# A hybrid decoder layer on one core: one substitution for two, weight loads and subtractions moved between products

## The chip, the cores and the metric

The kernel runs on one core of a Trainium2 chip. A core has five engines that run their own instruction streams and wait for each other through semaphores: TensorE (PE in the profile; the unit that multiplies matrices, with its weight loads shown apart as PEld), VectorE (DVE), ScalarE (ACT), GpSimd (POOL) and SyncE (SP, which here issues DMAs). The metric is the device time of one execution in microseconds, the median of several runs. The kernel before has 1929.55 us, the median of three runs (1926.06, 1929.55 and 1931.4).

## The reference

One decoder layer over 1024 tokens with 1024 features, float32 throughout. Cut to its stages:

```python
u  = rmsnorm(h, norm_mix_pre)
qa, ka, va, za, ba, aa, ..., gnsa, gmix = split(u @ w_in)
ya = gdn_mixer(qa, ka, va, za, ba, aa, ...)   # chunked gated delta rule, 4 heads of 128
yb = nsa_mixer(...)                           # compressed, selected and window attention
g_a, g_b = split(sigmoid(gmix))
mixed = (g_a * (ya @ w_a2d) + g_b * (yb @ w_b2d)) @ w_o
h = h + rmsnorm(mixed, norm_mix_post)
f = causal_dwconv(rmsnorm(h, norm_ffn_pre) @ w_up) + conv_ffn_b
f_gate, f_val = split(f)
h = h + rmsnorm((gelu(f_gate) * f_val) @ w_down, norm_ffn_post)
h = h + rmsnorm((p @ w_ple) * sigmoid(h @ w_ple_gate), norm_ple_post)
```

In `gdn_mixer`, q, k and v pass a causal convolution of width 4 and a silu; q and k are normalised over each head. For every chunk and head a strictly lower triangular matrix L is formed, whose entry (i, j) is beta_i times k_i.k_j times exp(gc_i - gc_j), where gc is the running sum of the log decay. I + L is inverted (the reference solves with it), and the state runs over the chunks with the results. The kernel uses chunks of 128 tokens, eight in all, so there are 32 matrices L (eight chunks by four heads).

## The kernel before, in words

Almost every matrix product is done in three matmuls (`mm3`): each operand is kept as a rounded part hi and a remainder lo, and hi x hi, hi x lo and lo x hi are added up in PSUM. So each weight tile that is loaded by DMA (`raw`) needs two conversions before PE can use it: ACT copies it to hi, and DVE or POOL subtracts hi from raw for lo (`lo_of`, line 362). `stream` does that for the columns of a matrix, `resident` for the rows of w_o, `hl` for a tile that is in SBUF.

**The delta-net (GDN) stage**, some 60 to 285 us of the span. Twelve convolution tiles (`conv`; four of k, four of q, four of v) follow each other. Of each, PE makes 48 matmuls of 128x512 into a PSUM tile `pj`; ACT and DVE form the convolution `y` from it (one ACT pass, three DVE passes, line 573), and ACT the silu. After the q and k tiles, `norms` squares them on ACT and adds the squares over partitions by small products into `pss`. When the fourth k tile is there, `gdn_small` computes everything per token and head: beta, gc, the norms' factors, and rows of them that are spread over partitions through DRAM.

`gdn_inverse32` is a generator that is advanced once per convolution. Per chunk it scales k, calls `decay` (E = exp of the negated, clipped difference of gc: four DVE subtractions, line 948, and one ACT exponential, line 953), forms k k^T on PE (`pkk`), and L by two DVE passes (lines 984 and 985). L goes to DRAM, and its 32x32 diagonal blocks come back one on each partition (128 blocks: 32 matrices with four blocks each). All blocks are then inverted at once by forward substitution along the free axis: 31 columns, each one multiplication (line 1003) and one subtraction (line 1005). This is done in two halves: chunks 0 to 3, then their substitution on partitions 0 to 63, then chunks 4 to 7 and theirs on partitions 64 to 127. The inverses go to DRAM (`xd`), the tile is cleared (line 1011), and `gdn_prep` loads per chunk the inverted diagonal blocks and the off-diagonal blocks of L (`blk`) and builds the full inverse by products that depend on each other (`pz`, `pt` and so on).

Four gate tiles (`gate_tile`, 48 matmuls in two halves each, copied out by ACT as `yz`) come between the last convolution and `gdn_prep(0)`; sixteen more fill the scan over the chunks.

**The merge**, some 965 to 1025 us. For pairs of feature tiles f and both halves th of the tokens, PE multiplies yb by w_b2d into `pab` (`b_product`), and DVE forms ga*a + gb*b with gates read back from DRAM (`gt`). The result `mx` is kept as hi and lo. The next but one pair of w_b2d tiles is streamed at the end of each pair (its lo on POOL). Four of w_o's eight rows of tiles (`NWO`) are loaded ahead of the merge, the rest behind it. Then `token_mm` makes the output product `pwo` per tile of 128 tokens: tokens 0 to 2 with rows 0 to 3, then again with rows 4 to 7; the others all in one.

**The up- and down-projection** (1045 to 1800 us) use a scheme with seven products of half-size blocks in place of eight, with sums and differences of blocks formed by DVE and POOL. `UpProjection.rest` begins with the pairs 0 to 2 in an order written out by hand. `turn(t2s, 4, ...)` forms the operand T4 (a difference and a sum on DVE, hi on ACT, lo on DVE); `self.copied` is the last copy of a product out of PSUM by ACT, here that of the product named r (line 106). `block_sum` is a sum on POOL that the down-projection needs. In `down`, the products 0, 1, 6, 4 and 3 follow each other, each of eleven steps j with twelve matmuls (`dq`, `dm`, `dz`). Each step converts one activation tile (`whl`, lo on DVE) and one w_down tile (`wdhl`, lo on POOL). Beside product 4, DVE forms two differences per step for later products, lines 1567 and 1568.

What sets the order: the tile framework schedules each engine's instructions from the program's order and priorities; `issue_after` (and `behind`, line 1396, which nests several) puts what is issued inside it later than a named instruction in the queue of that instruction's engine. It does not wait for its end.

## Time and profile before

| | |
|---|---|
| runs | 1926.06, 1929.55, 1931.4 us; median 1929.55 |
| profiled execution | 1925.03 us, span 1923.3 us |
| mean granted clock of TensorE | 0.986 |
| busy PE, DVE, ACT, POOL | 95%, 65%, 48%, 36% of the span |
| DMA | 93 GB/s mean |

The profile's timeline gives one row per instruction or run of like instructions, with the start, the time and, in brackets, how long the engine was idle before it and what ended that. A granted clock below 1.0 in a stretch says that TensorE ran at the lower of its two levels (1.2 of 2.4 GHz) for a part of it. A name such as `pj<-uh,whi` is output from inputs; L394 is line 394.

### The profile page before, as it was taken

The numbers are of one execution on the slowest core, as the hardware profiler recorded it, in microseconds if no ns is written. First come the engines' busy times: TensorE is split into PE (matmuls) and PEld (weight loads), VectorE is DVE, ScalarE is ACT, GpSimd is POOL, SyncE is SP. The second block draws the span as 40 slices with busy tenths as digits, with TensorE's granted clock in tenths as the row PEclk, the third lists the DMA queues.
The fourth block names the chain that finished last, engine by engine and source line by source line (L and its number), as shares of the span: only waits on it lengthen the run. The fifth ranks groups of instructions, "written<-read, shape, count | busy, mean of one in ns | idle before, by whom it ended". The sixth has DMA issues, their size and how long they took to land. (4 is left out here: it accounts for less than half of the span.)

```text
span 1923.3 us, 25903 instructions
## 1 busy us (share of the span) xinstructions
PE 1834.8 (95%) x9307; PEld 1524.8 (79%) x9307; DVE 1242.5 (65%) x2353; ACT 919.2 (48%) x1817; POOL 700.2 (36%) x527
## 2 busy tenths in 40 slices
PE   7999989999999999999889998999999999899998
PEld 7888778988888888778768886787878877677786
DVE  5437934441367667766786589888777775948643
ACT  4344223323367667766664245444444444446432
POOL 2132112224122112331153146666666664645200
PEclk9999999999999999999999999999999999999999
DMA  5124333333310100110065212223332256246201
GB/s 168 34 86 116 91 92 89 93 88 92 102 45 18 45 29 34 57 44 13 22 216 169 98 55 94 98 94 101 107 99 93 99 206 243 77 138 219 76 34 44
DMA packets 182622, 178.67 MB, mean 93 GB/s; under 512 B 27549, under 2 KB 133342, under 8 KB 182494
## 3 DMA queue, kind: packets, MB, share of 16 engines
q1 hardware_dynamic: 180272, 170.33, 28.3%
q10 hardware_dynamic: 2222, 6.69, 0.9%
q8 instruction: 73, 1.20, 0.2%
q14 instruction: 55, 0.45, 0.1%
HBM read 132.65 MB, written 44.34 MB: 92 GB/s over the span
## 5 line engine op out<-in xcount | busy, mean ns | idle before, releaser
L394 PE MATMUL pj<-uh,whi 128*128 128x512 f32 x640 | 259.1, 405 | 7.4 <-DVE y L573 4.5
L395 PE MATMUL pj<-ul,whi 128*128 128x512 f32 x640 | 255.5, 399 | 0.0
L396 PE MATMUL pj<-uh,wlo 128*128 128x512 f32 x640 | 254.9, 398 | 0.0
L362 POOL TENSOR_TENSOR wlo<-raw,whi 128x1024 fp32r<-128x1024 f32 x48 | 117.5, 2449 | 312.1 <-ACT whi L373 268.3
L394 PEld LDWEIGHTS pj<-uh,whi 128*128 128x128 f32 x640 | 121.4, 190 | 35.4 <-issue 4.5
L362 POOL TENSOR_TENSOR whl<-s,whl 128x512 fp32r<-128x512 f32 x84 | 119.5, 1425 | 70.8 <-ACT whl L1393 69.0
L396 PEld LDWEIGHTS pj<-uh,wlo 128*128 128x128 f32 x640 | 121.2, 189 | 28.5
L395 PEld LDWEIGHTS pj<-ul,whi 128*128 128x128 f32 x640 | 121.4, 190 | 25.7
L362 POOL TENSOR_TENSOR whl<-raw,whl 128x512 fp32r<-128x512 f32 x71 | 114.6, 1621 | 62.6 <-ACT whl L1393 62.0
L362 POOL TENSOR_TENSOR wdhl<-wd,wdhl 128x512 fp32r<-128x512 f32 x66 | 100.0, 1524 | 82.2 <-ACT wdhl L1393 78.9
L362 DVE TENSOR_TENSOR whl<-araw,whl 128x512 fp32r<-128x512 f32 x77 | 89.8, 1173 | 54.9 <-ACT whl L1393 54.8
L394 PE MATMUL q<-mxh,whl 128*128 128x512 f32 (+1 forms) x272 | 105.9, 394 | 7.7 <-ACT r L106 7.7
L1275 ACT ACTIVATE Pt<-Pt,nm 128x640 f32<-128x640 f32 (+7 forms) x128 | 93.0, 729 | 36.4 <-DVE nm L1273 35.9
L1305 DVE TENSOR_TENSOR Tl<-pt,Th 128x512 fp32r<-128x512 f32 (+1 forms) x152 | 92.5, 616 | 21.7 <-ACT Th L1304 17.3
L396 PE MATMUL q<-mxh,whl 128*128 128x512 f32 (+1 forms) x272 | 105.1, 387 | 0.7 <-POOL whl L362 0.7
L395 PE MATMUL q<-mxl,whl 128*128 128x512 f32 (+1 forms) x272 | 105.3, 387 | 0.0
L1304 ACT ACTIVATE Th<-pt 128x512 fp32r<-128x512 f32 (+1 forms) x152 | 78.5, 539 | 42.7 <-PE po L1308 33.4
L373 ACT ACTIVATE whi<-raw 128x1024 fp32r<-128x1024 f32 x48 | 50.5, 1053 | 85.5 <-PE pj L395 55.5
L1301 PE MATMUL pt<-ident,Pt 128*128 128x128 f32 x528 | 83.4, 277 | 5.1 <-DVE Tl L1305 3.2
L1343 POOL TENSOR_TENSOR tm<-tm 128x128 f32<-128x128 f32 x32 | 14.8, 462 | 195.1 <-DVE tm L1341 155.3
L152 DVE SCALAR_TENSOR_TENSOR yg<-c,cv,yg 128x511 f32<-128x511 f32 (+2 forms) x88 | 76.9, 875 | 2.1 <-ACT yg L149 1.8
L152 DVE SCALAR_TENSOR_TENSOR yv<-c,cv,yv 128x1023 f32<-128x1023 f32 (+1 forms) x44 | 65.7, 1492 | 15.7 <-ACT yv L149 13.4
(548 smaller groups left out, 5181.4 us busy)
## 6 DMA issues: line engine op xcount, KB each, us to landing
raw<-in_w_up SPq DMA_DIRECT2D x44, 512.0 KB
raw<-in_w_in SPq DMA_DIRECT2D x40, 512.0 KB
araw<-acts SPq DMA_DIRECT2D x35, 512.0 KB
acts<-sd SPq DMA_DIRECT2D x44, 256.0 KB
gates_d<-yz SPq DMA_DIRECT2D x40, 256.0 KB
acts<-yv SPq DMA_DIRECT2D x33, 256.0 KB
gt<-gates_d SPq DMA_DIRECT2D x32, 256.0 KB
wd<-in_w_down SPq DMA_DIRECT2D x7, 1024.0 KB
```

The lines of the kernel that those rows point to most:

```text
L152: self.body.nc.vector.scalar_tensor_tensor(y, src, w, y, ALU.mult, ALU.add)
L362: return eng.tensor_sub(lo, src, hi.bitcast(F32)).ins
L373: nc.scalar.activation(hi, raw, AF.Copy)
L394: nc.tensor.matmul(ps, lh, rh, start=start, stop=False, skip_group_check=more)
L395: nc.tensor.matmul(ps, lh, rl, start=False, stop=False, skip_group_check=more)
L396: nc.tensor.matmul(ps, ll, rh, start=False, stop=stop, skip_group_check=more)
L1275: nc.scalar.activation(Pt[:, hh, 0:nk], Pt[:, hh, 0:nk], AF.Exp, scale=2.0 ** -(h0 + hh + 1), bias=nm[:, br, hh:hh + 1], accum_out=rs[:, b ...
L1301: nc.tensor.transpose(pt[:, b, hh], Pt[:, hh, (b0 + b) * P:(b0 + b + 1) * P], self.ident)
L1304: nc.scalar.activation(Th[:, 0:m], pt[:, 0:m], AF.Copy)
L1305: nc.vector.tensor_sub(Tl[:, 0:m], pt[:, 0:m], Th[:, 0:m].bitcast(F32))
L1343: nc.gpsimd.tensor_add(tm[:, 0], tm[:, 0], tm[:, 1])
```

## The change

The edits fall into four stretches of the program.

In the GDN stage, `gdn_small` is cut into three pieces that are issued behind the second and third convolution and behind the eighth (the two small parameter loads now come early, over ACT's queue); the strict decay is formed on ACT by four Relu with gc's negative as bias; L is formed in one pass of four DVE instructions (scalar_tensor_tensor), k k^T times beta times E; and one substitution over all 128 partitions, behind the eighth L, takes the place of the two. `gdn_prep(0)` is issued behind the second of the four gate tiles.

In the merge, `NWO` is 2, w_b2d's later tiles are streamed within the pair (behind the products of the second half of an odd f) with lo on DVE, and w_o's rows 2 to 7 are loaded behind the merge. The token products of tokens 0 to 2 go row by row for rows 0 to 3, then per token.

In `rest`, T4's conversion is also put behind the copy of r, and the first block sum is left to a later turn. In `down`, the difference of line 1568 moves from product 4 to product 3. No matmul is added or removed.

```diff
 NCMP = 64
-NWO = 4
+NWO = 2
...
         self.p5(b)
-        with body.behind(t3):
+        with body.behind(t3, self.copied):
             self.sums(b, (4,))
...
             def between():
-                if self.todo:
+                if self.todo and n > 2:
                     with body.behind(self.lo):
...
+                if t == 1:
+                    for i, name in enumerate(("a_log", "dt_bias")):
+                        nc.scalar.dma_start(self.adb[:, i * H:i * H + H], rows_to_all(io[name], H))
...
-            if i == 7:
-                self.gp = self.g1 = self.pool(ges, "gdn")
-                self.gdn_small(pss[0][:, 0, 0:NC * H])
...
-        inv = None
+        inv = small = None
...
             next(cv)
+            if inv:
+                with self.behind(last["DVE"], self.mm_last, *self.inv_last):
+                    next(inv, None)
             if n and order[n - 1] < 8:
                 norms(order[n - 1])
-            if order[n - 1] == 7:
-                inv = self.gdn_inverse32()
-            if inv:
-                next(inv, None)
             run_all(cv)
-        run_all(inv)
+            if n == 1:
+                self.gp = self.g1 = self.pool(ges, "gdn")
+                small = self.gdn_small(pss)
+            if n in (1, 2):
+                with self.behind(*last.values(), self.mm_last):
+                    next(small)
+            if order[n - 1] == 7:
+                run_all(small)
+                inv, self.inv_last = self.gdn_inverse32(), ()
+        with tc.issue_after(last["DVE"]):
+            run_all(inv)
...
         for n in range(4):
             run_all(gate_tile(n))
+            if n == 1:
+                with tc.issue_after(self.mm_last):
+                    self.gdn_prep(0)
         NG = 8
-        self.gdn_prep(0)
...
                     run_all(b_product(pm2, wb, f, th))
+                if th and f % 2 and f0 + 4 < KD:
+                    wbs.append(self.stream(wbd, 0, 4, (f0 + 4) * P, 2 * P, nc.vector))
                 nc.vector.tensor_mul(gb, ps0.pop(), gb)
...
-            if f0 + 4 < KD:
-                wbs.append(self.stream(wbd, 0, 4, (f0 + 4) * P, 2 * P))
...
-        al = t32("al", H)
-        nc.sync.dma_start(al, rows_to_all(io["a_log"], H))
-        db = t32("db", H)
-        nc.sync.dma_start(db, rows_to_all(io["dt_bias"], H))
+        al, db = self.adb[:, 0:H], self.adb[:, H:2 * H]
...
         nc.vector.scalar_tensor_tensor(v3(g), v3(ln), -1.0, hb(ea), ALU.mult, ALU.mult)
+        yield
         ps = self.psgt("pgc")
...
         nc.vector.tensor_copy(gc, ps[:, 0, 0:n])
+        ngc = self.ngc = k32("ngc")
+        nc.vector.tensor_scalar(ngc, ps[:, 0, 0:n], -1.0, None, ALU.mult)
         gam = t32("gam")
         nc.scalar.activation(gam, gc, AF.Exp)
-        rk = self.rsqrt(kss, "rk")
+        yield
+        rk = self.rsqrt(kss[0][:, 0, 0:NC * H], "rk")
...
         for h in range(H):
-            nc.vector.tensor_scalar(E[:, h], gr[:, h], self.gc[:, c * H + h:c * H + h + 1], 0.0, ALU.subtract,
-                                    ALU.min if causal else ALU.max)
+            j = slice(c * H + h, c * H + h + 1)
+            if causal:
+                nc.vector.tensor_scalar(E[:, h], gr[:, h], self.gc[:, j], 0.0, ALU.subtract, ALU.min)
+            else:
+                nc.scalar.activation(E[:, h], gr[:, h], AF.Relu, bias=self.ngc[:, j])
...
-        for hf in range(2):
-            for c in range(hf * NC // 2, (hf + 1) * NC // 2):
...
-                E = self.decay(c, gr, False)
-                L = self.g1.tile([P, H, P], F32, name="L", tag="Z", bufs=2)
-                nc.vector.tensor_mul(L, pk, E)
-                nc.vector.tensor_mul(L, L, self.bc(self.beta[:, c * H:(c + 1) * H]))
...
-            m_ = hn * 4
-            pp = slice(hf * m_, hf * m_ + m_)
...
-            for j in range(31):
-                m, w = 31 - j, j + 1
-                t = tmp[pp, 0:m * w].rearrange("p (a b) -> p a b", b=w)
-                nc.vector.tensor_mul(t, Ls[pp, j + 1:, j].unsqueeze(2).to_broadcast([m_, m, w]),
-                                     X_[:, j, 0:w].unsqueeze(1).to_broadcast([m_, m, w]))
-                nc.vector.tensor_sub(X_[:, j + 1:, 0:w], X_[:, j + 1:, 0:w], t)
-                if j in (12, 20):
-                    yield
-            nc.sync.dma_start(self.xd[0, pp], X_)
-            nc.vector.tensor_copy(Ls[pp], X_.rearrange("p i j -> p j i"))
-            nc.sync.dma_start(self.xd[1, pp], Ls[pp])
+        for c in range(NC):
...
+            E = self.decay(c, gr, False)
+            L = self.g1.tile([P, H, P], F32, name="L", tag="Z", bufs=2)
+            for h in range(H):
+                j = c * H + h
+                self.inv_last = (nc.vector.scalar_tensor_tensor(L[:, h], pk[:, h], self.beta[:, j:j + 1], E[:, h],
+                                                                ALU.mult, ALU.mult).ins,)
...
+        for j in range(31):
+            m, w = 31 - j, j + 1
+            t = tmp[:, 0:m * w].rearrange("p (a b) -> p a b", b=w)
+            nc.vector.tensor_mul(t, Ls[:, j + 1:, j].unsqueeze(2).to_broadcast([P, m, w]),
+                                 X[:, j, 0:w].unsqueeze(1).to_broadcast([P, m, w]))
+            nc.vector.tensor_sub(X[:, j + 1:, 0:w], X[:, j + 1:, 0:w], t)
+            if j in (8, 15, 22):
+                yield
+        nc.sync.dma_start(self.xd[0], X)
+        nc.vector.tensor_copy(Ls, X.rearrange("p i j -> p j i"))
+        nc.sync.dma_start(self.xd[1], Ls)
...
     def open_wo(self, es):
-        self.wo = self.resident(self.pool(es, "woA"), "w_o", range(NWO))
+        self.wo = self.resident(self.pool(es, "woA"), "w_o", range(NWO), (self.nc.vector,))
...
-        for k in (range(NWO), range(NWO, n))[half]:
+        for k in ks:
             mh, ml = [m[:, k % 4, s] for m in self.mx[k // 4, t // 4]]
...
-        for ks, tag in (((4, 5), "raw"), ((6,), "hi"), ((7,), "lo")):
+        for ks, tag in (((2, 3), "raw"), ((4, 5), "hi"), ((6, 7), "lo")):
             self.wo += self.resident(wb, "w_o", ks, place=(self.wp, tag))
...
-        for half in range(2):
+        for k in range(4):
             for t in range(3):
-                product(t, half)
+                product(t, (k,))
+        for t in range(3):
+            product(t, range(4, KD))
...
-                for half in range(2):
-                    product(t + 3, half)
+                product(t + 3, range(KD))
...
                 nc.vector.tensor_sub(b12[:, j], b22[:, j], b12[:, j])
-                nc.vector.tensor_sub(b21[:, j], b21[:, j], t2[:, j])
         for t in range(4):
             nc.scalar.activation(facc[:, 4 + t, c0], Q[t], AF.Copy)
-        run(product(3, b11, Q, False))
+        for j in product(3, b11, Q, False):
+            with self.behind(up.lo):
+                nc.vector.tensor_sub(b21[:, j], b21[:, j], t2[:, j])
```

What the order of instructions on DVE is in the GDN stage, where L is formed. Before, two of the chunks 4 to 7; `tmp` and `blk` are the first half's substitution, E the decay, y a convolution:

```order
L984 TENSOR_TENSOR L<-pkk,E 128x512
L573 SCALAR_TENSOR_TENSOR y<-pj,cvw,y 128x1022
L1005 TENSOR_TENSOR blk<-blk,tmp 64x20x12
L985 TENSOR_TENSOR L<-L,beta 128x512
L948 TENSOR_SCALAR E<-row_1427,gc 128x128 x4
L573 SCALAR_TENSOR_TENSOR y<-pj,cvw,y 128x1021
L1003 TENSOR_TENSOR tmp<-blk 64x247
L984 TENSOR_TENSOR L<-pkk,E 128x512
L1005 TENSOR_TENSOR blk<-blk,tmp 64x19x13
```

Now, at chunks 0 to 3:

```order
L1006 SCALAR_TENSOR_TENSOR L<-pkk,beta,E 128x128 x4
L574 SCALAR_TENSOR_TENSOR y<-pj,cvw,y 128x1023
L1006 SCALAR_TENSOR_TENSOR L<-pkk,beta,E 128x128 x4
L1000 TENSOR_TENSOR kT<-kT,row_1136 128x4x128
L1000 TENSOR_TENSOR kT<-kT,row_1162 128x4x128
L574 SCALAR_TENSOR_TENSOR y<-pj,cvw,y 128x1022
L574 SCALAR_TENSOR_TENSOR y<-pj,cvw,y 128x1021
L1006 SCALAR_TENSOR_TENSOR L<-pkk,beta,E 128x128 x8
```

The two passes over L and the four pieces of E that stood on DVE are one row of four instructions a chunk (x8 is two chunks), and no substitution row stands between them.

What stands on PE at the first product on the inverse, pz. Before (pj are the last gate products ahead of it and the first behind it):

```order
L395 MATMUL pj<-ul,whi 128x512
L396 MATMUL pj<-uh,wlo 128x512
L961 MATMUL pz_2025<-blk 128x128 x4
L961 MATMUL pt_2032<-Z,blk 128x128 x4
L1041 MATMUL pt1n<-ident,TT 128x128 x4
L961 MATMUL pqk<-qT,kT 128x128 x4
L961 MATMUL pz_2068<-TT,blk 128x128 x4
L1059 MATMUL pkt<-ident,kT 128x128 x4
L1064 MATMUL pvt<-ident,vT 128x128 x4
L961 MATMUL pt_2088<-Z,T_2038 128x128 x4
L961 MATMUL pz_2152<-blk 128x128 x4
L961 MATMUL pu<-vT,T_2087 128x128 x4
```

Now:

```order
L394 MATMUL pj<-uh,whi 128x512
L395 MATMUL pj<-ul,whi 128x512
L982 MATMUL pz_1853<-blk 128x128 x4
L396 MATMUL pj<-uh,wlo 128x512
L394 MATMUL pj<-uh,whi 128x512
L395 MATMUL pj<-ul,whi 128x512
```

and 17 gate products further on:

```order
L395 MATMUL pj<-ul,whi 128x512
L396 MATMUL pj<-uh,wlo 128x512
L982 MATMUL pt_1860<-Z,blk 128x128 x4
L394 MATMUL pj<-uh,whi 128x512
L395 MATMUL pj<-ul,whi 128x512
```

pz stands within the third gate tile, and 22 gate products lie between it and pt, which needs its result; before, the ten small products followed each other.

What DVE does in the down-projection's product 4 (wd and wdT hold blocks of w_down and their differences, whl is an activation tile). Before:

```order
L362 TENSOR_TENSOR whl<-araw,whl 128x512
L1567 TENSOR_TENSOR wd_14426<-wd_14424,wd_14426 128x512
L1568 TENSOR_TENSOR wd_14425<-wd_14425,wdT_14423 128x512
L362 TENSOR_TENSOR whl<-araw,whl 128x512
L1567 TENSOR_TENSOR wd_14426<-wd_14424,wd_14426 128x512
L1568 TENSOR_TENSOR wd_14425<-wd_14425,wdT_14423 128x512
L362 TENSOR_TENSOR whl<-araw,whl 128x512
```

Now, the end of product 4 and the start of product 3:

```order
L1588 TENSOR_TENSOR wd_14378<-wd_14376,wd_14378 128x512
L362 TENSOR_TENSOR whl<-araw,whl 128x512
L1588 TENSOR_TENSOR wd_14378<-wd_14376,wd_14378 128x512
L362 TENSOR_TENSOR whl<-araw,whl 128x512
L1593 TENSOR_TENSOR wd_14377<-wd_14377,wdT_14375 128x512
L362 TENSOR_TENSOR whl<-araw,whl 128x512
L1593 TENSOR_TENSOR wd_14377<-wd_14377,wdT_14375 128x512
```

A step of product 4 has two rows in place of three, and a step of product 3 two in place of one.

## Rows read from the trace of the kernel before

**Rows 1.** The page's first lines: span; busy us, share, instructions of PE.
```profile
span 1923.3 us, 25903 instructions
...
PE 1834.8 (95%) x9307; PEld 1524.8 (79%) x9307; DVE 1242.5 (65%) x2353; ACT 919.2 (48%) x1817; POOL 700.2 (36%) x527
```

**Rows 2.** Timeline of PE, GDN stage: start, us, engine, line, operation; in brackets idle, releaser.
```profile
72.79 0.47 PE L394 MATMUL pj<-uh,whi 128*128 128x512 f32 x1 [2.15 <-DVE y L573]
...
143.11 2.08 PE L961 MATMUL pkk<-kT 128*128 128x128 f32 x8 [1.11 <-DVE L L984]
...
215.50 0.47 PE L394 MATMUL pj<-uh,whi 128*128 128x512 f32 x1 [1.55 <-DVE y L573]
...
234.80 0.63 PE L394 MATMUL pj<-uh,whi 128*128 128x512 f32 x1 [2.26 <-ACT yz L611]
...
268.00 1.13 PE L961 MATMUL pz<-blk 128*128 128x128 f32 x8 [3.39 <-DMA blk<-ld]
```

**Rows 3.** Six stretches: length, busy us (instructions) by engine, granted clock, DMA share, GB/s.
```profile
143.00:156.00 13.00, 12.89 (x48) 11.28 (x49) 10.14 (x20) 3.34 (x5) 0.00 (x0) 0.61 0.60 176
234.00:239.00 5.00, 4.20 (x11) 3.31 (x12) 4.79 (x7) 1.24 (x3) 2.36 (x1) 0.66 0.30 71
266.00:278.00 12.00, 8.53 (x49) 8.02 (x50) 3.10 (x8) 2.48 (x5) 2.59 (x2) 0.72 0.49 129
994.00:1000.00 6.00, 3.75 (x10) 2.97 (x11) 5.96 (x6) 5.19 (x8) 4.67 (x3) 0.53 0.90 306
1156.00:1164.00 8.00, 6.77 (x17) 5.34 (x18) 7.63 (x11) 5.37 (x8) 3.50 (x2) 0.57 0.24 69
1682.00:1690.00 8.00, 6.29 (x17) 4.95 (x18) 1.76 (x2) 1.15 (x2) 5.40 (x4) 0.57 0.20 68
```

**Rows 4.** Timelines of DVE and ACT, GDN stage, in order of time.
```profile
118.24 1.28 ACT L574 ACT_TABLE_LOAD   x1 [2.81 <-DVE y L573]
119.53 1.06 ACT L574 ACTIVATE qT<-y 128x1024 f32<-128x1024 f32 x1
...
131.40 0.87 DVE L948 TENSOR_SCALAR E<-row,gc 128x128 f32<-128x128 f32 x4 [1.56 <-DMA row<-rows_d]
...
132.31 0.63 ACT L953 ACTIVATE E<-E 128x512 f32<-128x512 f32 x1 [2.62 <-DVE E L948]
...
142.38 0.68 DVE L984 TENSOR_TENSOR L<-pkk,E 128x512 f32<-128x512 f32 x1
...
192.57 0.42 DVE L1003 TENSOR_TENSOR tmp<-blk 64x255 f32<-64x255 f32 x1
...
298.43 1.13 DVE L1090 SCALAR_TENSOR_TENSOR r<-pw,bg,vT 128x128 f32<-128x128 f32 x4
```

**Rows 5.** Timelines of PE and DVE, end of the merge and first token products.
```profile
996.25 0.80 PE L394 MATMUL pab<-ybh,whi 128*128 128x512 f32 x1 [5.75 <-ACT whi L373]
...
1020.26 0.39 PE L394 MATMUL pwo<-w_oh,mxh 128*128 128x512 f32 x1
1020.49 0.39 PE L395 MATMUL pwo<-w_ol,mxh 128*128 128x512 f32 x1
...
1023.18 0.68 DVE L818 TENSOR_TENSOR gt<-pab,gt 128x512 f32<-128x512 f32 x1
```

**Rows 6.** Timeline of PE, opening of the up-projection.
```profile
1157.23 0.80 PE L394 MATMUL q<-mxh,whl 128*128 128x512 f32 x1 [2.79 <-ACT r L106]
...
1210.75 0.50 PE L394 MATMUL n<-T4h,whl 128*128 128x512 f32 x1 [2.48 <-DVE c L179]
```

**Rows 7.** Timelines of POOL, DVE and PE, down-projection, in order of time.
```profile
1674.64 9.01 POOL L362 TENSOR_TENSOR wdhl<-wdT,wdhl 128x512 fp32r<-128x512 f32 x1 [4.10 <-ACT wdhl L1393]
...
1681.85 0.68 DVE L1568 TENSOR_TENSOR wd<-wd,wdT 128x512 f32<-128x512 f32 x1
...
1683.70 0.80 PE L395 MATMUL dq<-wdhl,whl 128*128 128x512 f32 x1 [5.72 <-POOL wdhl L362]
...
1688.29 1.28 POOL L362 TENSOR_TENSOR wdhl<-wdT,wdhl 128x512 fp32r<-128x512 f32 x1 [2.17 <-ACT wdhl L1393]
```

More of the change, by code (lines that the diff above doesn't have):

```diff
@@ L395, in mm3 @@
         nc.tensor.matmul(ps, lh, rl, start=False, stop=False, skip_group_check=more)
-        nc.tensor.matmul(ps, ll, rh, start=False, stop=stop, skip_group_check=more)
+        self.mm_last = nc.tensor.matmul(ps, ll, rh, start=False, stop=stop, skip_group_check=more).ins
     def rstd_of(self, ss, n, scale, name):
@@ L491, in mixers @@
         self.cvw = keep.tile([P, 81], F32, name="cvw")
+        self.adb = keep.tile([P, 2 * H], F32, name="adb")
         ges = ExitStack()
@@ L572, in conv @@
                 d = 3 - j
-                nc.vector.scalar_tensor_tensor(y[:, d:], ps[:, 0:SEQ - d], cwt(j), y[:, d:], ALU.mult, ALU.add)
-            nc.scalar.activation(qkvT[i], y, AF.Silu)
+                last["DVE"] = nc.vector.scalar_tensor_tensor(y[:, d:], ps[:, 0:SEQ - d], cwt(j), y[:, d:], ALU.mult,
+                                                             ALU.add).ins
+            last["ACT"] = nc.scalar.activation(qkvT[i], y, AF.Silu).ins
+        last = {}
         order = [4, 5, 6, 7, 0, 1, 2, 3, 8, 9, 10, 11]
-        inv = None
+        inv = small = None
         for n, i in enumerate(order):
@@ new lines, in gdn_inverse32 @@
+        for c in range(NC):
+            rk = self.row4(1, c, "qk", 2)
+            gr = self.row4(0, c, "gr", 2)
+            k = self.chunk(1, c)
+            nc.vector.tensor_mul(k, k, rk)
+            E = self.decay(c, gr, False)
+            pk = self.mm4(self.psgt("pkk"), k, k)
+            L = self.g1.tile([P, H, P], F32, name="L", tag="Z", bufs=2)
[3 more added lines that the diff above has]
+                                                                ALU.mult, ALU.mult).ins,)
+            nc.sync.dma_start(self.ld[c], L)
+            for h in range(H):
+                p0 = (c * H + h) * 4
+                l = self.ld
+                nc.sync.dma_start(Ls[p0:p0 + 4], bass.AP(
+                    tensor=l.tensor, offset=l.offset + (c * P * H + h) * P,
+                    ap=[[32 * H * P + 32, 4], [H * P, 32], [1, 32]]))
+            if c % 2:
+                yield
@@ L1429, in ffn, with product @@
         pw, t2s = {}, []
-        def product(t, half):
-            if half == 0:
+        def product(t, ks):
+            if ks[0] == 0:
                 pw[t] = [bank("pwo") for _ in range(2)]
-            self.token_mm(pw[t], t, self.wo, half)
+            self.token_mm(pw[t], t, self.wo, ks)
         def turned(t, xs):
```

26 lines of the change are left out of this document (6 added, 20 removed).

## The prediction

> **What bounds the kernel now.** The page's first part was read first: TensorE (PE) is busy for 1834.8 of 1923.3 us [rows 1]. The other engines do not set the time by their sums, so a change that removes no matmul, and this one removes none, can give back two things only: the 88.5 us in which PE stands (1923.3 - 1834.8), and the time in which it runs below its full clock. The second view was PE's own timeline, for every gap above half a microsecond with what released it. Nine of them, in the four stretches that the diff touches, carry the sum: five in the delta-net (GDN) stage [rows 2], one in the merge [rows 5], two in the up-projection's opening [rows 6], one in the down-projection [rows 7]. The third view was the table of stretches around them [rows 3]: behind each longer gap the granted clock is between 0.53 and 0.72, which mixes the two levels, 1.2 and 2.4 GHz. I price what the clock costs as PE's busy time there times what is missing to 1.0: 12.89 x 0.39 = 5.0 us at 143 to 156, 4.20 x 0.34 = 1.4 at 234 to 239, 8.53 x 0.28 = 2.4 at 266 to 278, 3.75 x 0.47 = 1.8 at 994 to 1000, 6.77 x 0.43 = 2.9 at 1156 to 1164, 6.29 x 0.43 = 2.7 at 1682 to 1690. The gap of 1.55 us at 215.50 has no such tail. The fourth view was the timelines of VectorE (DVE), ScalarE (ACT) and GpSimd (POOL) in these stretches, to see what each releaser had been doing.
>
> **GDN stage, the instructions.** Removed on DVE: per chunk, for eight chunks, the four strict-decay subtractions, 0.87 us, and two passes over L of 0.68 us; added: four scalar_tensor_tensor that read PSUM, as the nearest group of four of that size does, 1.13 us [rows 4]. That is 0.87 + 2 x 0.68 - 1.13 = 1.1 us a chunk, 8.8 us in all. The two substitutions of 62 instructions on 64 partitions become one of 62 on 128, with the same widths; the longest of one takes 0.42 us [rows 4], so at most 62 x 0.42 = 26 us of DVE go. Added on ACT: four Relu of 128x128 a chunk. No such row exists; one exponential over the same 512 elements takes 0.63 us [rows 4], so four lie between 0.63 and 4 x 0.63 = 2.5 us; I take 0.8, because on DVE four pieces cost 0.87 where one whole costs 0.68. Times eight, 6.4 us (5 to 20). The order also has four table loads more, each of 1.28 us [rows 4], 5.1 us. ACT is busy 3.34 us of the 13 at 143 to 156 [rows 3], so this has room beside PE, unless its order makes it late (a rival below).
>
> In the trace the load at 118.24 is over at 119.52 and the silu behind it begins at 119.53 [rows 4]. The Trainium skill (ScalarE: Activation LUTs, What ACT_TABLE_LOAD costs) puts a switch at 1283 ns plus a drain of about 1380 ns, 2.66 us together; by that, four would cost an estimated 10.6 us of ACT. The 1283 ns agree with this trace; a drain on top is not to be seen there, so the trace's 5.1 us stand in the sum.
>
> **GDN stage, the gaps.** (a) 72.79, 2.15 us: the products wait for DVE's convolution y, which stands behind the gate preparation (gdn_small) in one piece. It now comes in three pieces behind two convolutions, and the two loads at its head are early. The DVE work is the same, so not all of it goes: 1.5. (b) 143.11, 1.11 us, with the 5.0 of clock: a cluster of tiny products (the k k^T of two chunks and the column sums) all at one place, waiting for L. In the new order they are spread over four places and L takes 1.1 us less; but two pairs still stand close together: 4.0 of 6.1. (c) 215.50, 1.55 us, for y behind the first substitution's rows: 1.2. (d) 234.80, 2.26 us with 1.4 of clock: ACT's copy yz stood behind a silu that waited for the last y on DVE, again behind substitution rows. DVE is lighter there: 2.3 of 3.7. (e) 268.00, 3.39 us with 2.4 of clock: the first product on the inverse (pz) waits for the block's DMA, and the small products behind it, most of which need each other, follow bare. By the new order the last k k^T stands 48 conv products earlier, and pz has 58 gate products fewer ahead of it, which now stand between the dependent steps. At a pitch of 0.23 us [rows 5] the data come 48 x 0.23 = 11.0 us earlier and PE 58 x 0.23 = 13.3 us earlier; so the wait becomes 3.39 + 13.3 - 11.0 = 5.7 us less what DVE saves ahead of the end of the substitution (up to 26 us by its instructions), that is nothing to 5.7. I take 0.5 for it; the bare chain and its clock go, the wait mostly: 4.0 of 5.8. The sum is 1.5 + 4.0 + 1.2 + 2.3 + 4.0 = 13.0 us, of 19.3 that are there; the low end, all of (e) lost and half the rest, is 4.
>
> **Merge.** At 996.25 PE waits 5.75 us for whi of w_b2d, whose load is issued behind sixteen gate loads and two of w_o; its clock tail is 1.8: 7.5 in all. The load now follows eight gate loads, and two rows of w_o go behind the merge. What is late next is DVE: it is busy 5.96 of 6 us at 994 to 1000 [rows 3], and it gets the lo parts of two streamed tiles from POOL. The last product with the gates ends on DVE at 1023.18 + 0.68 = 1023.86, 3.6 us behind the first token product at 1020.26 [rows 5]. Token 1's banks are two of the last ones that DVE empties. Before, they were wanted after token 0's 24 matmuls, 5.5 us; now after 6, 1.4 us. So up to 2.2 us of wait, and some clock, come at the new place, and DVE's extra parts push it out by as many again. I take 7.5 - 5.5 = +2; bounds -1 and +6. The rows of w_o that are now loaded later are wanted, by the pitch, no sooner than their conversion; priced at nothing, covered by 18 matmuls a row, 4.1 us.
>
> **Up-projection's opening.** The 2.79 us at 1157.23 and 2.9 of clock [rows 3, 6]: ACT's copy r stood behind three conversions T4h that wait for DVE. Behind the copy, as they now are, PE gets r at once. But DVE is busy 7.63 of 8 us there [rows 3], the work is only put off, and 53 us later PE waits 2.48 us for DVE's c [rows 6]; that wait takes what the first gives, but for the clock in part: +1 (-2 to +5). The block sums skipped for the first pair come some POOL operations later, beside nothing that waits.
>
> **Down-projection.** At 1683.70 PE waits 5.72 us, and 2.7 of clock, for one POOL subtraction that took 9.01 us where the next takes 1.28 [rows 7]. DVE ran three subtractions a step back to back until 1681.85 + 0.68 = 1682.53, and POOL's ended 1.1 us behind. Eleven of these (0.68 us and up) move to the next product, where DVE has only the whl parts. Eleven x 0.68 = 7.5 us at least: DVE would run dry about that much sooner, and POOL's turn comes 7 of its 7.7 us of delay sooner. I take 6.5 of 8.4 (0 to 9).
>
> The Trainium skill (SBUF — State Buffer, Who interferes with whom) says that a DVE instruction with two SBUF inputs and a GpSimd instruction that reads SBUF exclude each other for whole instructions, and it speaks against this part: the moved subtractions would block POOL one product later. The row of 9.01 us agrees with the rule, so it is the first rival below.
>
> **Sum.** 13 + 2 + 1 + 6.5 = 22.5 us off the profiled execution's 1925.03 gives 1902.5. That execution was 4.5 us under the median of the runs, 1929.55; on the median it is 1907. All low ends together make 4 - 1 - 2 + 0 = 1 us, all high ends 19.3 + 6 + 5 + 9 = 39.3; neither is likely, since the four stretches are far apart.
>
> **Rivals.** (1) The late engine stays late: in the down-projection POOL's subtraction starves beside the moved work, the merge's wait reappears whole at token 1's banks, r gives nothing. Of GDN's 13 some 11.5 remain: 1918. (With POOL's part alone it is 1907 + 6.5 = 1913.5, inside the forecast's own range.) For it: DVE's shares in rows 3; against: in the next product DVE has two subtractions a step, 1.4 us, in a step of 12 matmuls, 2.8 us, so there are holes. (2) The GDN gain fails, the rest works: one E tile serves all chunks, so each chunk's Relu waits for the last L, and weights and y queue behind it on ACT; GDN +2, others 9.5: 1918 too. For it: the two places in ACT's order where whi stands behind a Relu; against: ACT's room. (3) Slower: the joint substitution starts only when all eight L are there, where half of it used to run before. If the E chain (0.8 + 1.28 + 0.63 + 1.13 = 3.8 us a chunk, 31 us for eight, against three convolutions of 48 products, 33 us) slips by two chunks and the substitution's rows are then spread between the last y, pz gets its data 20 us later than PE comes: 20 + 3 of clock - 5.8 there before = 17 us lost, 9 gained at (a) to (d), none elsewhere: 1938. With the other gains as forecast (9 + 9.5) it makes the kernel slower from 24 us of wait and clock on, with none outside GDN from 15. (4) The change moves waits only and nothing is left: 1928.
>
> **How the numbers follow.** Forecast 1907 (its own range 1896 to 1914): 0.50. Rivals (1) and (2): 0.20 and 0.12. Rival (4): 0.09; rival (3): 0.09. A measurement of this kernel cannot tell less than about 0.3%, 5.8 us, from no change: under 1923.8 is faster, 0.50 + 0.32 less 0.02 that lie above it: 0.80. Same 0.11, slower 0.09. The range of 8 in 10: 1893 to 1924.
>
> **What would show it.** Right: no gap above 2 us on PE between 130 and 285 us and a clock of 0.9 or more there; the wait for whi in the merge gone, a smaller one at the second token's pwo; r's wait gone and a larger one at c; no POOL subtraction above 4 us in the down-projection. Wrong: a long wait at the first pz; Relu rows that wait for L with whi behind them; a long POOL subtraction one product later; a bank wait of 5 us or more behind the merge.

## The result and the profile after

The changed kernel takes 1908.89 us, the median of four runs (1902.9 to 1911.54), against 1929.65 us; the ratio is 0.989 (95% interval 0.9863 to 0.9918), so it is faster by 20.8 us. Measured again (median of six runs): 1905.68 us, ratio 0.9895 (0.9875 to 0.9916). The prediction was 1907. The page's head, to set beside [rows 1]:

```profile
span 1901.2 us, 25847 instructions
...
PE 1826.6 (96%) x9307; PEld 1516.6 (80%) x9307; DVE 1211.1 (64%) x2276; ACT 935.4 (49%) x1853; POOL 686.6 (36%) x524
```

PE's idle time fell from 88.5 to 74.6 us; the remaining 8 us of the span's 22.1 are PE rows that got shorter at the same number of matmuls, while the mean granted clock rose from 0.986 to 0.992. The timeline of PE at the places of [rows 2], [rows 5] and [rows 6] (start, us, engine, line, operation; idle and releaser):

```profile
73.69 0.47 PE L394 MATMUL pj<-uh,whi 128*128 128x512 f32 x1 [1.11 <-DVE y L574]
...
91.41 0.41 PE L921 MATMUL pgc<-small,triu 128*128 128x32 f32 x2 [0.96 <-DVE small L918]
...
211.74 0.48 PE L394 MATMUL pj<-uh,whi 128*128 128x512 f32 x1 [0.77 <-DVE y L574]
...
245.25 1.13 PE L982 MATMUL pz<-blk 128*128 128x128 f32 x8 [2.01 <-DMA blk<-ld]
...
1004.02 0.50 PE L394 MATMUL pwo<-w_oh,mxh 128*128 128x512 f32 x1 [2.10 <-DVE gt L837]
...
1146.77 0.50 PE L396 MATMUL m<-mxh,whl 128*128 128x512 f32 x1 [2.90 <-POOL whl L362]
...
1162.62 0.80 PE L394 MATMUL n<-T4h,whl 128*128 128x512 f32 x1 [2.87 <-DVE c L179]
...
1194.17 0.50 PE L394 MATMUL n<-T4h,whl 128*128 128x512 f32 x1 [2.18 <-DVE c L179]
...
1750.41 1.21 PE L396 MATMUL dn<-wdhl,whl 128*128 128x512 f32 x4 [2.11 <-DVE whl L362]
```

Of the GDN stage's waits, 72.79 and 215.50 are half there, those at 143 and 234.80 are gone, and pz waits 2.01 us at 245.25 where it waited 3.39 at 268.00. A wait of 0.96 for the gates' small sums is new. Behind the first pz three more waits are gone that [rows 2] does not show, and that the forecast did not count as waits. In the kernel before:

```profile
269.82 2.08 PE L961 MATMUL pt<-Z,blk 128*128 128x128 f32 x8 [0.69 <-ACT Z L1034]
...
272.68 1.11 PE L1041 MATMUL pt1n<-ident,TT 128*128 128x128 f32 x4 [0.78 <-DVE TT L1037]
...
279.96 1.13 PE L961 MATMUL pz<-blk 128*128 128x128 f32 x8 [1.44 <-DMA blk<-xd]
```

In the merge the wait for whi is gone and one for a bank that DVE empties (gt) has come. In the up-projection the wait for r is gone, and waits of 2.90, 2.87 and 2.18 us for whl and c stand there, 8.0 us together; before, four waits (2.79 for r, 1.32 and 2.48 for c, 1.73 for whl) made 8.3. In the down-projection's products 4 and 3 no wait is left; one of 2.11 us for whl stands in the product behind them, where one of 0.88 us was. The stretches that answer to [rows 3] (length, busy us by engine, granted clock, DMA share, GB/s):

```profile
137.00:150.00 13.00, 13.00 (x75) 11.41 (x75) 7.06 (x14) 11.47 (x17) 2.35 (x1) 0.87 0.62 179
228.00:233.00 5.00, 5.00 (x23) 4.04 (x22) 3.31 (x10) 0.60 (x1) 0.15 (x1) 1.00 0.34 132
243.00:265.00 22.00, 19.99 (x116) 17.03 (x114) 3.92 (x11) 7.71 (x12) 3.09 (x3) 1.00 0.45 117
1000.00:1010.00 10.00, 7.54 (x26) 5.42 (x25) 7.25 (x11) 3.73 (x5) 0.00 (x0) 0.83 0.49 164
1160.00:1168.00 8.00, 5.38 (x17) 4.36 (x18) 7.80 (x9) 3.94 (x7) 3.63 (x3) 0.79 0.31 100
1655.00:1675.00 20.00, 20.00 (x87) 16.05 (x87) 16.81 (x19) 10.07 (x18) 9.81 (x8) 1.00 0.37 117
```

The whole GDN stage in the same columns, from the last of the products `psm` ahead of it to the first product `pS` of the scan over the chunks, before and now:

```profile
62.88:286.21 223.33, 209.19 (x993) 172.73 (x992) 139.42 (x265) 85.24 (x97) 51.81 (x22) 0.95 0.33 90
64.81:271.00 206.19, 201.08 (x993) 166.15 (x992) 105.50 (x185) 98.35 (x132) 51.07 (x22) 0.99 0.35 96
```

PE runs as many matmuls; it stands for 5.1 us in place of 14.1, and is busy for 8.1 us less at the higher clock. So half of the stage's gain is waiting and half is clock.

At single places, the clock that cost 5.0 us in the cluster costs 13.00 x 0.13 = 1.7; behind the first pz it is full; in the merge a tail of 7.54 x 0.17 = 1.3 us lies behind the new wait, and 5.38 x 0.21 = 1.1 behind c. The new instructions, and POOL's subtraction in the down-projection, beside [rows 4] and [rows 7] (ACT, ACT, ACT, DVE, POOL):

```profile
133.48 1.28 ACT L970 ACTIVATE E<-row,ngc 128x128 f32<-128x128 f32 x4 [4.25 <-DMA row<-rows_d]
...
136.72 1.28 ACT L576 ACT_TABLE_LOAD   x1
138.01 1.06 ACT L576 ACTIVATE qT<-y 128x1024 f32<-128x1024 f32 x1
...
139.86 1.13 DVE L1006 SCALAR_TENSOR_TENSOR L<-pkk,beta,E 128x128 f32<-128x128 f32 x4 [2.72 <-PE pkk L982]
...
1670.30 1.29 POOL L362 TENSOR_TENSOR wdhl<-wd,wdhl 128x512 fp32r<-128x512 f32 x1 [1.52 <-ACT wdhl L1412]
```

Four Relu take 1.28 us (0.8 had been taken, between 0.63 and 2.5), four scalar_tensor_tensor 1.13 as priced, a table load 1.28. By the Trainium skill (ScalarE: Activation LUTs, What ACT_TABLE_LOAD costs) a switch costs 1.38 us of drain on top of the load. None is seen here: the row before the load at 136.72 ends at 136.70, and the silu at 138.01 begins 1.29 us after the load did.

Where the time came from, by stage: the length of each stage in a run's trace less its length in the kernel before. GDN is from the last `psm` to the first `pS`, attention to the first `pab`, merge to the first `q` of the up-projection, up to the first `dz`, down to the first `pi`. All runs of this study, in us against the kernel before (one profiled execution each):

| run | GDN | attention | merge | up | down |
|---|---|---|---|---|---|
| the change | -17.1 | +1.3 | -1.4 | +0.4 | -7.3 |
| after_again | -17.9 | +5.2 | -1.6 | +0.9 | -9.8 |
| gdn_alone | -16.2 | +4.1 | -3.7 | -0.5 | +0.1 |
| merge_alone | +1.4 | -0.4 | -3.3 | -0.3 | +0.5 |
| rest_alone | +0.6 | +5.2 | +0.2 | +0.4 | +0.6 |
| down_alone | -2.2 | -1.3 | -0.5 | -0.3 | -8.4 |
| gdn_and_down | -16.2 | +2.6 | -3.7 | +2.6 | -9.2 |
| pairs_no_rest | -14.1 | +3.2 | -3.0 | +0.7 | -9.4 |
| late_prep | -13.9 | -0.6 | -2.6 | +0.3 | -9.2 |
| order_021 | -17.1 | +3.9 | -4.4 | +0.5 | -8.9 |
| psum_subs | -0.4 | +1.8 | -1.0 | +0.9 | -8.2 |
| split_subst | +4.5 | -2.0 | -3.0 | +2.3 | -7.0 |
| dve_decay | -16.9 | +1.1 | -1.1 | +0.2 | -8.0 |

A stage that a run does not touch scatters by 1 to 2.6 us, and attention by more: from -2.0 to +5.2. Stages with the same new code differ as much: GDN is 14.1 to 17.9 us shorter in the six traces with its whole part, and the merge 1.1 to 3.0 in the five with its part as the change has it (the change, after_again, late_prep, split_subst, dve_decay). Ahead of the GDN stage, where the table does not begin, the change is 1.9 us later than the kernel before; merge_alone and psum_subs, which edit nothing there, are 1.5 us later too. The traces that are late there have a stretch at the lower clock near 25 us (granted 0.72 from 24 to 30 in the change, 1.00 before), the others have none.

### The profile page after: what moved, and what is told of

Same layout as the page of the kernel before. It is cut to its first block, busy times and chain, and to the rows that moved or that the text cites. A ratio compares the mean times of both kernels' runs of the same rounds, so it can differ in the third digit from the quotient of the medians.

```text
span 1901.2 us, 25847 instructions
## 1 busy us (share of the span) xinstructions
PE 1826.6 (96%) x9307; PEld 1516.6 (80%) x9307; DVE 1211.1 (64%) x2276; ACT 935.4 (49%) x1853; POOL 686.6 (36%) x524
## 4 chain that ended last, share of the span: by engine, by line
PE 74%; DVE 11%; issue 5%; DMA 3%; ACT 3%; POOL 3%; SPq 1%; POOLq 0%; DVEq 0%; ACTq 0%
PE pj L394 6%; PE pj L396 6%; PE pj L395 6%; PE q L394 3%; PE q L396 3%; PE q L395 3%; PE pt L1320 2%; PE ps L1286 2%; PE n L394 2%; PE dq L395 2%; PE n L395 2%; PE n L396 2%; PE pg L396 2%; PE dq L396 2%; PE dq L394 2%
## 5 line engine op out<-in xcount | busy, mean ns | idle before, releaser
L362 POOL TENSOR_TENSOR wlo<-raw,whi 128x1024 fp32r<-128x1024 f32 x46 | 110.9, 2413 | 302.2 <-ACT whi L373 249.3
```

Of the source, the lines that this page charges most:

```text
L362: return eng.tensor_sub(lo, src, hi.bitcast(F32)).ins
```

## The experiments

**The four parts alone**, each put into the kernel before; the edits are those of the diff, by function.

```
gdn_alone:   mixers, gdn_small, decay, gdn_inverse32, gdn_prep's place
merge_alone: under, open_wo, token_mm, the products of ffn
rest_alone:  "behind(t3, self.copied)" and "self.todo and n > 2"
down_alone:  b21 -= t2 in product 3
```

> The kernel before with the GDN part alone. By the two traces the GDN stage gave 15.4 us (scan's first product pS at 286.21 before, 271.00 after, and 1.9 us later at its start), so theory 1 (the parts are independent and add up) expects 1929.6 - 15.5 = 1914, with pz near 245 and no gap over 2.5 us between 130 and 285. The rival (the parts' gains share one reserve, or the profiled run of after was a lucky one, 6 us under its median) expects 1918 to 1922.

Measured: 1909.59 us, ratio 0.9911 (0.9896 to 0.9926), 17 us; the GDN stage 16.2 us shorter, and its waits are those of the whole change. The rival falls, and the total is 4 us lower than theory 1 expected. Not expected was the merge, whose code is unchanged here, but 3.7 us shorter. Its waits in PE's timeline, with the two of the up-projection's opening:

```profile
984.23 0.50 PE L394 MATMUL pab<-ybh,whi 128*128 128x512 f32 x1 [1.14 <-DVE gt L835]
...
1143.16 0.50 PE L394 MATMUL q<-mxh,whl 128*128 128x512 f32 x1 [2.76 <-ACT r L106]
...
1164.03 0.50 PE L394 MATMUL n<-T4h,whl 128*128 128x512 f32 x1 [2.87 <-DVE c L179]
```

The wait of 5.75 us for whi [rows 5] is gone. In the order of SP's queue the third load of w_b2d stands behind fifteen gate loads where it stood behind sixteen; it is issued 15.8 us behind the first pab (970.90) where it was 18.6 (984.07), and ACT's whi follows at 977.32 where it came at 995.16, behind a copy that waited for DVE. So the framework's scheduler placed the merge's instructions anew, though only the GDN stage was edited. Which of these differences makes the gap go was not tried by itself.

> The kernel before with the merge part alone. Theory 1: the wait of 5.75 us for whi at 996 goes, a wait of 2 to 3 us for a bank comes at the seventh token product, with a clock tail: 1929.6 - 1.5 = 1928. Rival (the wait at the banks costs all that was won, or the later rows of w_o are late too): 1930 to 1933.

Measured: 1926.51 us, ratio 0.9988 (0.9979 to 0.9998), 2.3 us; the stage 3.3 us shorter, and a wait of 2.42 us for a bank at the seventh token product. This is what theory 1 expects, and the rival falls. But GDN alone gives the merge as much without this edit; with both, 1.4 and 1.6 us are left in two traces.

> The kernel before with the opening of the up-projection alone. Theory 1 (DVE sets this stretch): the wait for r goes, waits of 2 to 3 us for whl's lo on POOL and for c on DVE take its place; 1929.6 + 0.7 = 1930. Rival (the wait for r was worth its 2.8 us and clock, and what took its place in the kernel after came from the other parts): 1925 to 1927.

Measured: 1930.99 us, ratio 1.0011 (0.9997 to 1.0026): no gain, and the rival falls. The waits in this stretch of PE's timeline:

```profile
1171.63 0.50 PE L394 MATMUL n<-T3h,whl 128*128 128x512 f32 x1 [1.20 <-ACT whl L1393]
...
1184.51 0.79 PE L394 MATMUL n<-T4h,whl 128*128 128x512 f32 x1 [3.97 <-DVE c L179]
...
1216.96 0.50 PE L394 MATMUL n<-T4h,whl 128*128 128x512 f32 x1 [1.68 <-DVE c L179]
```

The wait for r, 2.79 us in [rows 6], is gone; those for whl and c are 1.20, 3.97 and 1.68 us.

> The kernel before with the down-projection part alone. Theory 1: no POOL subtraction above 4 us in products 4 and 3, the waits of 5.72 and 0.75 us go with their clock tail (9.5 us by the traces), a wait of 2 us for whl comes back in the product after; 1929.6 - 7.5 = 1922. Rival (POOL is locked out one product later by the moved subtractions): a POOL subtraction of 4 us or more in product 3, and 1927 to 1930.

Measured: 1919.03 us, ratio 0.9955 (0.9937 to 0.9973), 8.7 us; the stage 8.4 us shorter. The longest POOL subtraction of w_down in products 4 and 3 takes 1.77 us. The stretch of product 4 in which the wait stood (columns as in [rows 3]):

```profile
1665.00:1690.00 25.00, 25.00 (x108) 20.13 (x107) 19.77 (x21) 11.91 (x21) 11.53 (x9) 1.00 0.35 101
```

PE is busy throughout at full clock. The rival, POOL locked out one product later, falls.

**The whole against its parts.**

> The changed kernel again, with more rounds, beside the next three on the same chip. The four parts alone gave ratios of 0.9911, 0.9988, 1.0011 and 0.9955, whose product is 0.9865, 1902.5. Theory 1 (the parts add up): 1903 to 1905. Theory 2 (the merge's wait for whi is gone already once the GDN part shifts the stage, as in the trace of GDN alone, where the merge gave 3.7 us with its old code against 1.4 us with the new code in the kernel after, so that the merge part then costs 2 us and the first part of rest 1 to 2): 1907 to 1909.

Measured as told above, 1905.68 us: between the two theories, and its interval does not tell them apart. The next run does so better.

> The kernel before with the GDN and the down part, the merge and the opening of the up-projection as before. Theory 1 (all parts add up): 0.9911 x 0.9955 x 1928 = 1902.3, 0 to 2 us above the whole change. Theory 2 (merge and opening cost in company with GDN): about 1901, 4 to 6 us under the whole change; pab to q in the merge 3 us shorter than before, without a wait for whi above 2 us.

Measured: 1905.69 us, ratio 0.9891 (0.9874 to 0.9907), the same as the whole change beside it. So the merge and the opening together give nothing that the totals can tell once the other two parts are there (the intervals are some 3 to 4 us to each side). The loss that theory 2 expected in the total is not seen either; by stage the merge is 2.1 to 2.3 us shorter with its old code (-3.7 against -1.4 and -1.6), about the scatter of a stage. Its old code does not run free of waits here. As expected there is none for whi, but DVE is late:

```profile
981.82 0.50 PE L394 MATMUL pab<-ybh,whi 128*128 128x512 f32 x1 [2.84 <-DVE gt L835]
```


Why totals tell so little below 4 us: attention, which none of these edits touches, was up to 5.2 us longer from trace to trace, and in two traces of the same kernel it differs by 3.9 us. The whole of it and two stretches, in after_again:

```profile
540.00:545.00 5.00, 4.56 (x16) 3.71 (x17) 3.74 (x17) 3.42 (x14) 0.91 (x2) 0.66 0.00 0
820.00:825.00 5.00, 4.55 (x20) 3.94 (x20) 1.26 (x8) 4.38 (x10) 2.52 (x2) 0.66 0.00 0
270.28:954.66 684.38, 660.53 (x3962) 566.03 (x3961) 390.47 (x1252) 379.82 (x951) 160.99 (x161) 0.99 0.18 54
```

and in the change, which is the same kernel:

```profile
540.00:545.00 5.00, 4.44 (x23) 3.59 (x23) 4.25 (x19) 3.03 (x13) 0.92 (x2) 1.00 0.00 0
820.00:825.00 5.00, 4.78 (x26) 3.49 (x25) 3.82 (x16) 4.93 (x13) 1.51 (x2) 1.00 0.00 0
271.00:951.51 680.51, 656.58 (x3962) 562.00 (x3961) 390.53 (x1252) 379.76 (x951) 161.09 (x161) 1.00 0.19 55
```

In both PE stands for 23.9 us. The 3.9 us are all in its busy time: the two short stretches run at full clock in the one trace and at 0.66 in the other.

**The wait that came in the merge.**

```diff
-        for k in range(4):
-            for t in range(3):
-                product(t, (k,))
-        for t in range(3):
-            product(t, range(4, KD))
+        for ks in ((0, 1), (2, 3), range(4, KD)):
+            for t in range(3):          # order_021: (0, 2, 1), the banks allocated before the loop
+                product(t, ks)
```

Both runs leave out the edits in `rest`.

> The changed kernel without the opening of the up-projection's part, and with the token products of tokens 0 to 2 by rows 0 and 1 together, then 2 and 3 (12 matmuls a token, 2.8 us, before token 1's banks are wanted). If the 2.1 us wait at 1004 with its clock tail is a wait for banks that come free at 1003.96 and 1005.29, a later want takes at least 1.4 us of it and the half clock behind it: the merge part 2.5 to 3.5 us shorter than in the changed kernel, and in all 1903 to 1905. Rival (the wait only moves to token 2's banks or to row 2 of w_o): no shorter, 1907.

Measured: 1900.64 us, ratio 0.986 (0.9845 to 0.9876); merge -3.0. The total is lower than expected, but the merge is only some 1.5 us shorter than in the change, and the wait is not gone:

```profile
1007.70 0.80 PE L394 MATMUL pwo<-w_oh,mxh 128*128 128x512 f32 x1 [2.81 <-DVE gt L837]
```

It stands where token 1 begins, now behind twelve token products. The row of DVE that ends it is itself later here: it is over 5.7 us behind the first token product (1007.65 less 1001.99), in the change 3.6 (1003.96 less 1000.37). So a later want did not help by as much as it was later.

> The kernel of the run pairs_no_rest, with the tokens of its first three products in the order 0, 2, 1 (their banks as before). There the wait stood at token 1's first product, 2.81 us at 1007.70, 12 matmuls after the first token product. If it is a wait for the two banks that DVE empties last, token 1 now comes after 24 matmuls, 5.6 us, and the wait and its half clock go: pab to q 3 to 4 us shorter than in pairs_no_rest, 1897 to 1898 in all. Rival (token 2's banks are no sooner free, or the time is given back at w_o's rows): the same wait at token 2, 1900 to 1901.

Measured: 1899.4 us, ratio 0.9832 (0.981 to 0.9855), the lowest median of the study (the interval of dve_decay overlaps); merge -4.4. Token 1, now behind 24 products, waits no more; what is left are the starts of token 2's two halves, behind twelve:

```profile
1004.90 0.50 PE L394 MATMUL pwo<-w_oh,mxh 128*128 128x512 f32 x1 [0.58 <-DVE gt L837]
...
1006.22 0.50 PE L394 MATMUL pwo<-w_oh,mxh 128*128 128x512 f32 x1 [0.35 <-DVE gt L837]
```

with no half clock behind them (granted 1.00 from 998 to 1010). The stage gained 1.4 us on pairs_no_rest where 3 to 4 were expected, which is within the scatter of this stage. What ends token 2's two waits are DVE's last two rows for `pab` (over at 1004.84 and 1006.17), as it was for token 1 in the change (1003.96 and 1005.29). So whichever token comes second waits for the last two banks, as the rival says; it is shorter than in the change because it stands behind twelve products and not six, and shorter than in pairs_no_rest because the first of the two rows is over 3.4 us behind the first token product and not 5.7.

**What in the GDN part gives the time.**

```diff
late_prep:
-            if n == 1:
-                with tc.issue_after(self.mm_last):
-                    self.gdn_prep(0)
         NG = 8
+        self.gdn_prep(0)
split_subst:
+        for hf in range(2):      # memset, 31 columns, stores on partitions 64*hf to 64*hf + 63
dve_decay:
-                nc.scalar.activation(E[:, h], gr[:, h], AF.Relu, bias=self.ngc[:, j])
+                nc.vector.tensor_scalar(E[:, h], gr[:, h], self.gc[:, j], 0.0, ALU.subtract, ALU.max)
```

> The changed kernel with the first chunk's preparation behind all four gate tiles, as before. By term (e) of the prediction, the data come some 11 us earlier than before and PE 13 us later than in the changed kernel, so no wait for the block's DMA is left, but the chain of dependent small products stands bare: 1.5 to 3 us of gaps between pz and pu, and a half clock behind them of 1 to 3 us: 3 to 5 us slower than the changed kernel. Rival (the place does not matter once the substitution is joint): within 1 us.

Measured: 1903.52 us, ratio 0.9878 (0.9862 to 0.9895), not slower in the total, where 3 to 5 us were expected; in the stage -13.9 against -17.1 and -17.9. The chain's waits are back:

```profile
259.58 1.16 PE L980 MATMUL pt<-Z,blk 128*128 128x128 f32 x8 [1.27 <-ACT Z L1051]
...
261.52 1.12 PE L1058 MATMUL pt1n<-ident,TT 128*128 128x128 f32 x4 [0.78 <-DVE TT L1054]
...
268.95 1.16 PE L980 MATMUL pu<-vT,T 128*128 128x128 f32 x8 [0.68 <-DVE T L1084]
```

Not all of these 3 to 4 us belong to the chain. Some lie at the front of the stage, where the code is that of the change and the clock is not; the change first, then late_prep:

```profile
86.00:100.00 14.00, 13.04 (x66) 10.83 (x66) 8.88 (x19) 8.33 (x11) 2.35 (x1) 1.00 0.14 39
86.00:100.00 14.00, 13.05 (x54) 10.75 (x53) 8.76 (x19) 8.30 (x10) 2.35 (x1) 0.76 0.13 39
```

(pairs_no_rest, with the early preparation, has 0.76 there too, and -14.1 in the stage.) Behind the convolutions, from ACT's first copy yz of a gate tile to pS, it is 64.8 us in the kernel before, 55.8 here, and with the early preparation 53.3 to 53.4 in five of six traces and 54.9 in pairs_no_rest. So the early place is worth some 2.5 us in this one trace, under the 3 to 5 expected, and the totals cannot confirm it.

> The changed kernel with the one substitution over 128 partitions made as two over 64, both behind the last L. DVE's rows of the substitution took 29.8 us in the changed kernel (62 instructions, 188.42 to 230.46) and 53.0 us before (124). Theory 1 (the end of the substitution sets when the first pz can start, and the joint form is what hides it): pz comes 20 to 23 us later, PE waits that long for the block's DMA and runs at half clock behind it, 20 to 25 us slower, 1927 to 1931. Rival (DVE has slack until pz, because PE's gate products cover it): under 8 us.

Measured: 1921.19 us, ratio 0.9951 (0.9932 to 0.997), 12 to 15 us slower than the change, where 20 to 25 were expected; the GDN stage 21.6 us longer than in the change (+4.5 against -17.1).

```profile
247.89 0.50 PE L394 MATMUL pj<-uh,whi 128*128 128x512 f32 x1 [1.63 <-ACT yz L625]
...
272.52 2.05 PE L982 MATMUL pz<-blk 128*128 128x128 f32 x8 [13.16 <-DMA blk<-ld]
```

pz comes 27 us later. PE waits 13.16 us for the block's DMA, and 58 gate products more stand ahead of pz by the new order (13.3 us at a pitch of 0.23); the clock is 0.55 from 272 to 284. Theory 1 holds in kind, not in size: the end of the substitution sets pz, and behind the last L only the joint form ends in time.

> The changed kernel with the strict decay formed by four DVE subtractions again (0.87 us a chunk) in place of ACT's four Relu. Theory 1 (DVE sets the pace from the first L to the end of the substitution, and ACT has room): the last L some 3 to 7 us later, pz as much later, PE's wait there 2 + 3 to 7 us: 3 to 7 us slower, 1909 to 1913. Rival (the chain through the one E tile sets it, so that the place of the subtraction does not matter): pS within 1.5 us of the changed kernel.

Measured: 1900.33 us, ratio 0.9848 (0.9821 to 0.9874); GDN stage -16.9. Theory 1 falls: the last L ends 1.8 us later (182.60 against 180.77), and pz does not. pS comes 0.13 us later, within the rival's 1.5; that the chain through E is the reason was not tried.

```profile
200.43 0.47 PE L394 MATMUL pj<-uh,whi 128*128 128x512 f32 x1 [1.22 <-DVE y L574]
...
212.77 0.48 PE L394 MATMUL pj<-uh,whi 128*128 128x512 f32 x1 [0.91 <-DVE y L574]
...
245.38 1.13 PE L980 MATMUL pz<-blk 128*128 128x128 f32 x8 [1.11 <-DMA blk<-ld]
```

The waits for y are 1.22 and 0.91 us where one of 0.77 was, pz waits 1.11 where it waited 2.01. So the move of the decay to ACT is worth nothing that these traces show. That the total is 5 to 9 us under the change's two medians is explained by no stage of the trace.

**Why POOL took 9 us.** In the kernel before, with three DVE instructions a step as before:

```diff
-                nc.vector.tensor_sub(b12[:, j], b22[:, j], b12[:, j])
-                nc.vector.tensor_sub(b21[:, j], b21[:, j], t2[:, j])
+                nc.vector.tensor_sub(b12[:, j], b22[:, j], Z[j % 4])
+                nc.vector.tensor_sub(b21[:, j], b21[:, j], Z[j % 4])
```

> The kernel before, with the two differences that DVE forms beside product 4 of the down-projection reading their second operand from PSUM (a product's bank that is done with), so that each has one SBUF input; as many DVE instructions of the same size. The differences are then not those of the reference. Theory 1 (the POOL subtraction of 9.01 us was held off by DVE instructions with two SBUF inputs): the longest POOL subtraction in product 4 is under 3 us and the wait of 5.72 us goes or falls under 2 us; 8 us faster in this stretch. Rival (POOL's instruction was long, or PE late, because DVE had three instructions a step, whatever they read): the wait stays at 4 to 6 us.

Measured: 1919.69 us, ratio 0.9943 (0.9922 to 0.9963); down -8.2, as much as the move itself. DVE, POOL and DVE at the place of [rows 7], and the stretch around it in the kernel before and in this one (columns as in [rows 3]):

```profile
1671.30 0.67 DVE L1568 TENSOR_TENSOR wd<-wd,dz 128x512 f32<-128x512 f32 x1
1674.25 1.72 POOL L362 TENSOR_TENSOR wdhl<-wdT,wdhl 128x512 fp32r<-128x512 f32 x1 [1.78 <-DVE wd L1568]
1674.74 0.67 DVE L1567 TENSOR_TENSOR wd<-wd,dz 128x512 f32<-128x512 f32 x1
```

```profile
1660.00:1684.00 24.00, 17.54 (x73) 13.24 (x72) 22.52 (x29) 9.74 (x19) 16.80 (x7) 0.96 0.30 91
1660.00:1684.00 24.00, 23.79 (x101) 18.55 (x100) 22.44 (x31) 13.89 (x25) 14.22 (x10) 1.00 0.31 109
```

The longest POOL subtraction in products 4 and 3 takes 1.78 us, and no wait of PE above 0.6 us is left there. DVE is as busy as before, 22.44 us of 24 where it was 22.52. What held POOL off is DVE's second SBUF input, not DVE's load. The Trainium skill (SBUF — State Buffer, Who interferes with whom) has this rule, and this run agrees with it.

## Why the prediction was right, and where its steps were not

The total, 1907 against 1908.9 and 1905.7, is right, and the two parts that carry it are.

*GDN, 13.0 forecast, 14 to 18 measured.* (b) and (d) went as forecast or better: the cluster from 1.11 + 5.0 to 1.7, that is 4.4 won of 4.0 forecast, and 3.7 us to nothing, of which 2.3 had been forecast. (c) gave 0.8 of 1.2 (1.55 to 0.77). (a) failed: 2.15 us became 1.11 + 0.96 at two places, so 0.1 was won and not 1.5; cutting gdn_small into pieces moved its wait. (e) gave 3.8 of 5.8 at pz itself, where 4.0 had been forecast, but in another way: the wait for the block is 2.01 us and not 0.5, and the clock tail is gone whole. The five terms together measure 12.8 us. Most of what makes it 17.1 are waits that the sum left out: the bare chain was priced by its clock alone, and its gaps of 0.69, 0.78 and 1.44 us went too, and so did a wait of 0.78 us for y at 202.51. The count of DVE time was right for the substitution (29.8 us against 25.3 + 27.2, 23 saved, 26 the bound), whose joint form split_subst shows to be needed, and without effect for the decay. Of the stage's gain 11.5 us lie behind the first gate tile's copy, some 2.5 of them by the early preparation; which edit gives the rest ahead of it, the cluster's new places or the earlier substitution that is no longer there, was not tried by itself. The rival (2), a chain through E that starves ACT, did not come about.

*Merge, +2 forecast, 1.4 to 1.6 measured with all parts.* The mechanism went as written: whi's wait gone, 2.10 + 0.36 us at token 1's banks (up to 2.2 forecast) and 1.3 of clock. But the wait for whi was no property of the merge's code: GDN alone removed it. So the step that failed is the assumption that the four terms add up; gdn_alone's trace shows it, the totals do not (0.9865 by the product of the parts, 0.9895 measured, with an interval of 0.9875 to 0.9916).

*Up-projection, +1 forecast, 0 to -1 measured*: r's wait turned into waits for DVE and POOL; the later wait for c, which the forecast named, did not grow (2.48 to 2.18), but the earlier one did (1.32 to 2.87), and one of 2.90 us for whl came where 1.73 had stood at another product. Nothing was left over.

*Down-projection, 6.5 forecast, 7.3 to 9.8 measured* (8.4 alone): the whole wait with its clock, and one of 0.75 us ahead of it (1666.53); the wait of 2.11 us that came in the product behind is in the smaller figure and not in the larger. The term was undersized. That DVE's instructions held POOL off is shown by psum_subs, and that fewer of them a step free it by down_alone.

That the total fits so well is in part luck, since separate errors cancelled. In the change's own trace GDN is 4.1 us and the down-projection 0.8 us better than forecast; the merge is 0.6 and the opening 1.4 us worse, attention 1.3 and the stretch ahead of the GDN stage 1.9 us longer: 22.2 us for 22.5. Of the signs to look for, one was missed by little: pz's wait of 2.01 us is above the 2 us that were to be the limit between 130 and 285, and the clock was 0.87 from 137 to 150.

## What to carry to other kernels

Price a wait with its clock tail, and a chain of dependent small products with its gaps; then ask of each wait whether the code at that place makes it, or a schedule that any edit upstream may shift. Where GpSimd works beside VectorE, count VectorE's instructions with two SBUF inputs that run back to back, not its busy share. Read a change of a few us by stage, from matmul to matmul, when the stages beside it scatter as much.

## What had not been expected of the hardware

A POOL instruction was not only blocked by the DVE instruction that was running: it took 9.01 us across some thirteen DVE instructions of 0.68 us each without a gap between them, and ended 1.1 us behind the last. And equal stretches of attention ran at a granted clock of 1.00 or 0.66 in two executions of the same kernel, which made 3.9 us between them.
